# Wide matmuls over high and low x for z and three u products, state-space sums four heads at a time, scan tables two blocks at a time

## The chip, the core and the metric

The kernel runs on one core of a Trainium2 chip. The metric is the device time of one execution in microseconds. Three runs of the kernel before gave 1352.0, 1352.6 and 1353.1 us. The engines are TensorE (matmuls, in the profile PE and PEld), VectorE (DVE), ScalarE (ACT), GpSimd (POOL) and SyncE (SP, which issues most loads).

## What is computed

A decoder trunk of two layers over 256 positions of 2048 features, all in float32. Layer 0 has one input projection for two mixers, layer 1 a diagonal complex state-space mixer. Each layer ends in a residual with a layer norm. Cut to what matters here:

```
# layer 0
z, xbc, dt, q, k, v, gate = split(x @ w_in)           # z: 2048 features
xbc = silu(causal_depthwise_conv(xbc)); xs, bm, cm = split(xbc)
y   = ssd_scan(xs * dt, dt * a, bm, cm) + d_skip * xs  # 32 heads of 64 features
y_a = rms_norm(y * silu(z))
y_b = causal_attention(rotary(q), rotary(k), v) * silu(gate)   # 16 heads of 128
x   = layer_norm(alpha * x + concat(y_a, y_b) @ w_out)
# layer 1
u, gate = split(x @ w_in)                              # u: 2048 features
h_t = lam_bar * h_{t-1} + b_bar u_t                    # 128 groups of 16 channels, 64 complex states
y   = gelu(Re(C h) + d * u)
ga, gb = split(y @ w_glu)
x   = layer_norm(alpha * x + (ga * sigmoid(gb) * silu(gate)) @ w_out)
```

## The kernel before

**Products.** Nearly all the time goes into products with weights that are read once. A float32 operand is split into a high part (rounded to the matmul's replicated format, fp32r) and a low part (the rest), and a product is three matmuls: high by high, high by low and low by high. The weights come in 432 units of 512 KB (128 partitions x 1024 values: two k tiles of 512 columns). For each unit SyncE loads `raw`, ScalarE writes the high half `wh` (L230), VectorE the low half `wl` (L232). `raw`, `wh` and `wl` have four buffers each, and `split_to` is called three units ahead of the matmuls.

A "w" product (`wmm`, L297) has the weights as the stationary operand: per k tile and per 128 output features three matmuls with 256 columns, the positions, so its result is transposed (features on partitions). An "x" product (`xmm`, L276) has x stationary and 512 columns of weights moving. A product over 2048 features takes 8 units and yields 512 features, in two accumulator banks; `banks` gives two pairs in turn. B, C, xs, z, q, k, the attention gate and u are "w" products; v, the output projections, layer 1's gate and the gated unit are "x" products. The transposed x lies in two buffers, A (high) and B (low); later contents of the same kind lie in C and F.

**Other work between units.** After each unit `pump` runs jobs: `jobs` holds what the last product left to do (emptying accumulators among it), `back` holds long background work that is spread evenly over a range of units. `run` makes the instructions of a job come behind the weight splits of two units ahead on their engines. The order on each engine is at last set by a planner that simulates times when the kernel is compiled.

**State-space heads of layer 0.** `head_jobs(k)` for k = 0 to 15 treats two heads in five steps, and `skewed` runs the steps of neighbouring k staggered: `bcast` (L782: sums of log decays broadcast to all partitions by two matmuls), `decay` (ScalarE), `weigh` (VectorE), `apply` (L812, L813: the masked decay matrix times xs, full-precision float32, two heads side by side in the two 64-column halves of TensorE), `comb` (every second k: times SiLU of z). This begins in z's second product and ends in v's first.

**Tables of layer 1's scan.** `block_jobs(b)` for b = 0 to 15 makes tables from the parameters in the background of the attention and of the output projection: `bars`, `efs`, `fcs` on VectorE, `pes` (four transposes L715, eight small matmuls L719, a copy, a store to memory), `mts` on odd b (three matmuls L734).

**Layer 1.** u product 0 (`first1`) runs with the layer norm's tail. `u_store` copies a product's two banks to `ut` (ScalarE, L1104) and stores it; `u_load` brings it back in the scan's order; the scan (`enc` L1149, `rec1`, `rec2`, `dec` L1190 and L1194, `act`) runs in the background of the following products.

Of the kernel before, what the change touches and what calls it, by code (L numbers as in the profile page):

```python
# [16 lines left out]
P = 128  # L17
S = 256
# [3 lines left out]
CU = KT // UK  # L22
ALPHA = 4.0 ** 0.25
# [70 lines left out]

def _layout(inp):
# [22 lines left out]
    a["wi1"] = _chunk(f["in1_w"][0])  # L118
# [44 lines left out]
def trunk(tc, io, out):  # L163
# [8 lines left out]
    with ExitStack() as top:  # L172
# [98 lines left out]
        def xmm(ps, o, wpair, j, hk, start, stop):  # L271
            (xh, xl), k = hk
            wh, wl = wpair
            sl = slice(o * P, o * P + P)
            for i, (l, r) in enumerate(((xh, wh), (xh, wl), (xl, wh))):
                T.matmul(ps[o], l[:, k, sl], r[:, j, :], start=start and i == 0, stop=stop and i == 2)  # L276
# [3 lines left out]
        def wmm(ps, u, nu, hl, wpair, parts=WHOLE):  # L280
            pv = [p.rearrange("p (f n) -> p f n", n=S) for p in ps]
            wh, wl = wpair
            for part in parts:
                if callable(part):
                    part()
                    continue
                js, terms = part
                steps = [(j, o) for j in js for o in range(4)]
                if u == nu - 1:
                    steps = [(j, o) for o in range(4) for j in js]  # L290
                for j, o in steps:
                    first, end = u == 0 and j == 0, u == nu - 1 and j == UK - 1
                    (xh, xl), k = hl(u * UK + j)
                    sl = slice(o * P, o * P + P)
                    for i in terms:
                        l, r = ((wh, xh), (wh, xl), (wl, xh))[i]
                        T.matmul(pv[o // 2][:, o % 2, :], l[:, j, sl], r[:, k, :],  # L297
                                 start=first and i == 0 and o % 2 == 0, stop=end and i == 2 and o % 2 == 1,
                                 skip_group_check=True)

        def product(kind, hl, nu=CU, prelude=None, first=WHOLE):
# [15 lines left out]
            return ps  # L317

# [73 lines left out]
        xh = big("A", [P, KT, S], F32R)  # L392
        xl = big("B", [P, KT, S], F32R)
# [10 lines left out]
        with ExitStack() as l0:  # L404
# [35 lines left out]
            def xhl(k):  # L440
                return (xh, xl), k
# [103 lines left out]
            fmem = big("F", [P, 4096])  # L545
# [114 lines left out]
            ktp = [None]  # L660

            def block_jobs(b):
# [3 lines left out]
                def bars():  # L666
                    bc = h["bc"] = pp.tile([P, 4, 8, 16], F32, tag="bc", name=nm("bc"))
                    nc.sync.dma_start(bc.rearrange("p a g m -> p (a g m)"), io["s5bc"][b].rearrange("p a g m -> p (a g m)"))
                    bb = h["bb"] = pp.tile([P, 3, 8, 16], F32, tag="bb", name=nm("bb"))
# [10 lines left out]
                    V.tensor_scalar(bb[:, 2], bc[:, 2], nsg, None, op0=OP.mult)  # L680
# [7 lines left out]
                def efs():  # L688
                    bc, bb = h["bc"], h["bb"]
                    et = h["et"] = pp.tile([P, 8, 16, 4], F32, tag="et", name=nm("et"))  # L690
# [18 lines left out]
                def pes():  # L709
                    et, ob, bb = h["et"], h["ob"], h["bb"]  # L710
                    ev = et.rearrange("p (a i) m s -> p a (i m s)", i=2)
                    cv = bb[:, 2].rearrange("p (a i) m -> p a i m", i=2)
                    pe, pk = aux(), aux()
                    for a in range(4):
                        T.transpose(pe[:, a * P : a * P + P], ev[:, a, :], ident)  # L715
                    for a in range(4):
                        for i in range(2):
                            at = 64 * (i ^ (a % 2))
                            T.matmul(pk[at : at + 64, a * 16 : a * 16 + 16], ev[:, a, 64 * i : 64 * i + 64], cv[:, a, i, :], start=True, stop=True)  # L719
# [54 lines left out]
            def head_jobs(k):  # L774
# [40 lines left out]
                def comb():  # L815
                    if k % 2 == 1:
                        sv = sz[:, k - 1 : k + 1, :].rearrange("p f n -> p (f n)")
                        V.tensor_tensor(sv, d["y"], sv, op=OP.mult)
                        jk = c2([P, 2, S])
                        A.activation(jk.rearrange("p f n -> p (f n)"), sv, AF.Square)  # L820
                        for f in range(2):
                            G.tensor_tensor(ssq, ssq, jk[:, f, :], op=OP.add)

                return [bcast, decay, weigh, apply, comb]
# [53 lines left out]
            def attn_jobs(g, qT, kT, v, sg):  # L878
                for hp in range(2):
# [37 lines left out]
                    def pv(hp=hp, hold=hold):  # L917
# [8 lines left out]
                        if not yb:  # L926
                            yb["h"] = big("C", [P, KT, S], F32R)
                            yb["l"] = big("F", [P, KT, S], F32R)
# [32 lines left out]
            yah = big("A", [P, KT, S], F32R)  # L961
            yal = big("B", [P, KT, S], F32R)
# [11 lines left out]
            def mixhl(k):  # L974
                if k < 12:
                    return (yb["h"], yb["l"]), k
                if k < 28:
                    return (yah, yal), k - 12
                return (yb["h"], yb["l"]), k - 16

            def tailhl(k):
                return ((yb["h"], yb["l"]), k) if k < 16 else ((yah, yal), k - 16)
# [30 lines left out]
        with ExitStack() as lt:  # L1013
# [22 lines left out]
            def turned(t, f0, nf):  # L1036
                if not x1t:
                    x1t["h"] = big("C", [P, KT, S], F32R)
                    x1t["l"] = big("F", [P, KT, S], F32R)
# [42 lines left out]
            def x1hl(k):  # L1082
                return (x1t["h"], x1t["l"]), k
# [6 lines left out]
        with ExitStack() as l1:  # L1090
# [10 lines left out]
            def u_store(ps, j):  # L1101
                ut = w1("ut", [P, 4, S], 1)
# [118 lines left out]
            def y_split(j):  # L1221
                if j == 0:
                    y5["h"] = big("A", [P, KT, S], F32R)
                    y5["l"] = big("B", [P, KT, S], F32R)
# [13 lines left out]
            for j in range(8):  # L1238
                ps = product("w" if j < 4 else "x", x1hl) if j else first1
                if j < 4:  # L1240
                    jobs.append(lambda ps=ps, j=j: u_store(ps, j))
# [6 lines left out]
            def y5hl(k):  # L1248
                return (y5["h"], y5["l"]), k

            y2h = big("C", [P, KT, S], F32R)
            y2l = big("F", [P, KT, S], F32R)
# [24 lines left out]
            def y2hl(k):  # L1277
                return (y2h, y2l), k
# [7 lines left out]
        with ExitStack() as l2:  # L1286
            tp = l2.enter_context(tc.tile_pool(name="tp2", bufs=1))
            keep[0], keep[1] = tp, range(unit[0] + 2 * CU, unit[0] + 3 * CU)
            gb1 = big("A", [P, 2, D])
# [55 lines left out]
```

## Time and profile before

| | |
|---|---|
| runs before, us | 1352.0, 1352.6, 1353.1 (median 1352.6) |
| profiled execution, us | 1355.75 (span 1353.9, around it 1.85) |
| granted TensorE clock, mean | 0.996 |
| TensorE matmuls, loads of weights | 1337.0 us busy (99%), 1205.5 us (89%) |
| VectorE, ScalarE, GpSimd busy | 981.2 us (72%), 673.0 us (50%), 364.8 us (27%) |
| data moved | 283.01 MB, mean 209 GB/s |

One profiled execution is shown. Busy time of matmuls is the union of their modelled durations; since they are pipelined, the distance from one start to the next says what one costs. A group's row in the profile gives line, engine, operation, output and inputs by the program's names, shapes and count, then busy us and mean ns of one, then idle time of the engine before them and who ended it. A row of waits gives the engine and line that waited, whom it waited for, us in total, times, and the longest. In windows the five busy columns are PE, PEld, DVE, ACT, POOL, then the granted clock, the busy share of the DMA engines and GB/s.

### The profile page before, as it was taken

The numbers are of one execution on the slowest core, as the hardware profiler recorded it, in microseconds if no ns is written. First come the engines' busy times: TensorE is split into PE (matmuls) and PEld (weight loads), VectorE is DVE, ScalarE is ACT, GpSimd is POOL, SyncE is SP. The second block draws the span as 40 slices with busy tenths as digits, with TensorE's granted clock in tenths as the row PEclk, the third lists the DMA queues.
The fourth block names the chain that finished last, engine by engine and source line by source line (L and its number), as shares of the span: only waits on it lengthen the run. The fifth ranks groups of instructions, "written<-read, shape, count | busy, mean of one in ns | idle before, by whom it ended". The sixth has DMA issues, their size and how long they took to land.

```text
span 1353.9 us, 24904 instructions
## 1 busy us (share of the span) xinstructions
PE 1337.0 (99%) x9839; PEld 1205.5 (89%) x9839; DVE 981.2 (72%) x1560; ACT 673.0 (50%) x870; POOL 364.8 (27%) x648
## 2 busy tenths in 40 slices
PE   9999999999999999999999999999999999999996
PEld 8999999998998998998988888899988888888885
DVE  5767856787687879689787766748889856555556
ACT  5566567764544553554554334334444545444441
POOL 0041000122026528616798500022343100000001
PEclk9999999999999999999999999999999999999998
DMA  8655555545546756856767778497989766666762
GB/s 313 192 171 176 173 171 158 157 143 178 175 135 207 254 163 203 269 160 206 232 206 243 232 232 302 136 300 223 318 275 326 217 211 189 187 196 188 250 214 81
DMA packets 80741, 283.01 MB, mean 209 GB/s; under 512 B 9840, under 2 KB 12528, under 8 KB 80112
## 3 DMA queue, kind: packets, MB, share of 16 engines
q1 hardware_dynamic: 68112, 239.33, 56.2%
q0 software_dynamic: 7328, 30.42, 6.5%
q10 hardware_dynamic: 5184, 11.67, 2.3%
q8 instruction: 77, 1.26, 0.4%
q14 instruction: 40, 0.33, 0.1%
HBM read 260.41 MB, written 20.97 MB: 208 GB/s over the span
## 4 chain that ended last, share of the span: by engine, by line
PE 93%; DVE 4%; DMA 2%; issue 1%; ACT 0%; POOL 0%; SPq 0%; POOLq 0%; ACTq 0%; DVEq 0%
PE main L276 43%; PE main L297 42%; DVE wl L232 1%; PE aux L381 1%; PE aux L812 1%; PE aux L719 1%; PE enc L1149 1%; DMA bc<-in_s5bc 1%; PE dec L1194 1%; PE aux L924 1%; PE aux L892 1%; DMA ud<-ut 0%; PE aux L782 0%; PE dec L1190 0%; PE aux L715 0%
## 5 line engine op out<-in xcount | busy, mean ns | idle before, releaser
L232 DVE TENSOR_TENSOR wl<-raw,wh 128x1024 fp32r<-128x1024 f32 x431 | 538.4, 1251 | 323.4 <-ACT wh L230 317.4
L230 ACT ACTIVATE wh<-raw 128x1024 fp32r<-128x1024 f32 x431 | 455.8, 1059 | 580.3 <-PE main L276 269.2
L297 PE MATMUL main<-A,wh 128*128 128x256 f32 x1408 | 400.7, 285 | 1.3 <-ACT wh L230 1.1
L297 PE MATMUL main<-B,wh 128*128 128x256 f32 x1408 | 398.0, 284 | 0.0
L297 PE MATMUL main<-A,wl 128*128 128x256 f32 x1408 | 394.5, 283 | 0.0
L297 PEld LDWEIGHTS main<-A,wh 128*128 128x128 f32 x1408 | 269.7, 192 | 3.0 <-ACT wh L230 1.3
L297 PEld LDWEIGHTS main<-B,wh 128*128 128x128 f32 x1408 | 269.8, 192 | 0.4
L297 PEld LDWEIGHTS main<-A,wl 128*128 128x128 f32 x1408 | 267.8, 192 | 0.2 <-issue 0.2
L276 PE MATMUL main<-wl,A 128*128 128x512 f32 x512 | 200.5, 392 | 0.5 <-DVE wl L232 0.5
L276 PE MATMUL main<-wh,A 128*128 128x512 f32 x512 | 200.5, 392 | 0.0
L276 PE MATMUL main<-wh,B 128*128 128x512 f32 x512 | 199.9, 390 | 0.0
L276 PE MATMUL main<-wh,C 128*128 128x512 f32 x384 | 150.7, 393 | 0.0
L276 PE MATMUL main<-wh,F 128*128 128x512 f32 x384 | 149.8, 390 | 0.0
L276 PE MATMUL main<-wl,C 128*128 128x512 f32 x384 | 149.7, 390 | 0.0
L276 PEld LDWEIGHTS main<-wl,A 128*128 128x128 f32 x512 | 96.2, 188 | 21.3 <-DVE wl L232 1.8
L276 PEld LDWEIGHTS main<-wh,B 128*128 128x128 f32 x512 | 96.2, 188 | 19.9
L276 PEld LDWEIGHTS main<-wh,A 128*128 128x128 f32 x512 | 96.1, 188 | 19.8 <-issue 0.2
L653 POOL TENSOR_TENSOR c<-c 128x8 f32<-128x8 f32 (+2 forms) x192 | 106.7, 574 | 25.5 <-DMA wb<-c 18.0
L276 PEld LDWEIGHTS main<-wh,F 128*128 128x128 f32 x384 | 72.1, 188 | 15.3
L276 PEld LDWEIGHTS main<-wh,C 128*128 128x128 f32 x384 | 72.1, 188 | 15.1
L276 PEld LDWEIGHTS main<-wl,C 128*128 128x128 f32 x384 | 72.1, 188 | 14.6
L873 POOL TENSOR_TENSOR a<-a,b 64x512 f32<-64x512 f32 x16 | 28.2, 1769 | 169.1 <-DVE b L872 132.1
(279 smaller groups left out, 1651.6 us busy)
## 6 DMA issues: line engine op xcount, KB each, us to landing
raw<-in_wi SPq DMA_DIRECT2D x271, 512.0 KB, 4.0
raw<-in_wo SPq DMA_DIRECT2D x96, 512.0 KB, 4.3
raw<-in_wglu SPq DMA_DIRECT2D x64, 512.0 KB, 3.6
wt<-wb POOLq DMA_DIRECT2D x16, 896.0 KB, 6.9
wb<-ob ACTq DMA_DIRECT2D x16, 512.0 KB, 5.8
bc<-in_s5bc SPq DMA_DIRECT2D x16, 256.0 KB, 4.6
wb<-c POOLq DMA_DIRECT2D x16, 256.0 KB, 3.4
wb<-om ACTq DMA_DIRECT2D x16, 128.0 KB, 4.3
```

The lines of the kernel that those rows point to most:

```text
L230: high = A.activation(wh, raw, AF.Copy)
L232: splits[n] = (loaded[-1], high, V.tensor_tensor(wl, raw, wh.bitcast(F32), op=OP.subtract))
L276: T.matmul(ps[o], l[:, k, sl], r[:, j, :], start=start and i == 0, stop=stop and i == 2)
L297: T.matmul(pv[o // 2][:, o % 2, :], l[:, j, sl], r[:, k, :], start=first and i == 0 and o % 2 == 0, stop=end and i == 2 and o % 2 == 1, sk ...
L381: end = T.transpose(dst[:, i * P : i * P + P], s, ident)
L653: G.tensor_tensor(p[:, :, :, 0:m], cs[:, :, :, 1 : m + 1], cs[:, i, :, n : n + 1].unsqueeze(1).to_broadcast([P, 2, 4, m]), op=OP.mult)
L719: T.matmul(pk[at : at + 64, a * 16 : a * 16 + 16], ev[:, a, 64 * i : 64 * i + 64], cv[:, a, i, :], start=True, stop=True)
L812: T.matmul(yo, xs[:, 0, xc], df[:, i, 0:256], start=True, stop=False)
L873: turns.append(G.tensor_tensor(q[0:64], q[0:64], tm, op=OP.add))
L892: T.matmul(px[:, 128:384], qT[:, h, P:S], kT[:, h, :], start=True, stop=True)
L924: T.matmul(po, v[:, 0, hs], pT[:, i, 0:256], start=True, stop=False)
L1149: T.matmul(px[64 * at : 64 * at + 64, i, r * 128 + q * 64 : r * 128 + q * 64 + 64], wt[64 * i : 64 * i + 64, a * P + 64 * r : a * P + 64 * ...
```

## The change

It has four parts.

1. High and low x lie beside each other in one buffer, [128, 16, 2, 256] (`duo`): A holds what A and B held, C what C and F held. No amount of data changes.
2. z (four products) and u products 1 to 3 go through a new `product_wide`. A product is done in two halves of 256 output features. The weights of these products are stored in units of four k tiles by 256 columns, as large as before and as many. Per k tile and 128 features there are two matmuls: the high weight times 512 columns (high and low x), into both halves of a bank, and the low weight times high x, 256 columns, into the bank's second half. At the end of each half `total` copies the first half of the bank out (ScalarE) and adds the second (VectorE). z's SiLU then runs once per product, over 1024 columns; `u_store` only stores.
3. `apply` of an even k moves one step later, so that in every second step the products of four heads are issued together.
4. `pes` does nothing for even b; for odd b it does the transposes, the small matmuls, the copies and the stores of both blocks, with one accumulator and one pair of VectorE operations for the sixteen small results. `et` and the negated C table `cv` have two buffers.

```diff
+def _half(w):
+    k, n = w.shape
+    return w.reshape(k // (HK * P), HK, P, n // S, S).transpose(3, 0, 2, 1, 4).reshape(-1, P, HK * S)
...
-    cols = [xs, z]
+    cols = [_chunk(xs), _half(z)]
     for h in range(4):
-        cols += [m[:, 512 * h : 512 * h + 512] for m in (q, k, v, g)]
+        cols += [_chunk(m[:, 512 * h : 512 * h + 512]) for m in (q, k, v, g)]
     b, c = _chunk(b), _chunk(c)
     first = np.stack([b[:PAIRED], c[:PAIRED]], 1).reshape(-1, P, UK * 512)
-    a["wi0"] = np.concatenate([first, b[PAIRED:], c[PAIRED:]] + [_chunk(m) for m in cols], 0)
+    a["wi0"] = np.concatenate([first, b[PAIRED:], c[PAIRED:]] + cols, 0)
...
-    a["wi1"] = _chunk(f["in1_w"][0])
+    w = f["in1_w"][0]
+    a["wi1"] = np.concatenate([_chunk(w[:, 0:512]), _half(w[:, 512:2048]), _chunk(w[:, 2048:])], 0)
...
+        def product_wide(hl, dst, then):
+            for h in range(2):
+                ps = banks()
+                for u in range(HU):
+                    split_to(unit[0] + 3)
+                    wh, wl = (w.rearrange("p a n -> p (a n)").rearrange("p (k n) -> p k n", k=HK) for w in ready.pop(unit[0]))
+                    steps = [(j, o) for o in range(2) for j in range(HK)] if u == HU - 1 else [(j, o) for j in range(HK) for o in range(2)]
+                    for j, o in steps:
+                        first, end = u == 0 and j == 0, u == HU - 1 and j == HK - 1
+                        (xh, xl, xx), k = hl(u * HK + j)
+                        sl = slice(o * P, o * P + P)
+                        T.matmul(ps[o], wh[:, j, sl], xx[:, k, :, :].rearrange("p a n -> p (a n)"), start=first, stop=False, skip_group_check=True)
+                        T.matmul(ps[o][:, S : 2 * S], wl[:, j, sl], xh[:, k, :], start=False, stop=end, skip_group_check=True)
+                    unit[0] += 1
+                    pump(2 * HU - 1 - HU * h - u)
+
+                def total(o, ps=ps, h=h):
+                    to = dst()[:, 2 * h + o, :]
+                    A.activation(to, ps[o][:, 0:S], AF.Copy)
+                    V.tensor_tensor(to, to, ps[o][:, S : 2 * S], op=OP.add)
+
+                for o in range(2):
+                    run(lambda o=o: total(o))
+                then(h)
...
-        xh = big("A", [P, KT, S], F32R)
-        xl = big("B", [P, KT, S], F32R)
+        def duo(tag):
+            t = big(tag, [P, KT, 2, S], F32R)
+            return t[:, :, 0, :], t[:, :, 1, :], t
+
+        xh, xl, xx = duo("A")
...
+            fmem = cmem[:, 4096:8192]
...
-                    et, ob, bb = h["et"], h["ob"], h["bb"]
-                    ev = et.rearrange("p (a i) m s -> p a (i m s)", i=2)
-                    cv = bb[:, 2].rearrange("p (a i) m -> p a i m", i=2)
-                    pe, pk = aux(), aux()
-                    for a in range(4):
-                        T.transpose(pe[:, a * P : a * P + P], ev[:, a, :], ident)
-                    for a in range(4):
-                        for i in range(2):
-                            at = 64 * (i ^ (a % 2))
-                            T.matmul(pk[at : at + 64, a * 16 : a * 16 + 16], ev[:, a, 64 * i : 64 * i + 64], cv[:, a, i, :], start=True, stop=True)
-                    A.activation(ob[:, 0:512], pe, AF.Copy)
-                    if b % 2 == 0:
-                        ktp[0] = pp.tile([P, 8, 16], F32, tag="kt", name=nm("kt"))
-                    kt = ktp[0][:, 4 * (b % 2) : 4 * (b % 2) + 4, :]
-                    dc = PR("s5d")[:, 4 * b : 4 * b + 4].unsqueeze(2).to_broadcast([P, 4, 16])
-                    V.tensor_tensor(kt, C("kmask").unsqueeze(1).to_broadcast([P, 4, 16]), dc, op=OP.mult)
-                    V.tensor_tensor(kt, pk[:, 0:64].rearrange("p (a m) -> p a m", m=16), kt, op=OP.add)
-                    nc.scalar.dma_start(wb[b][:, 0:1024], ob)
+                    pair = [(b - 1, pend.pop()), (b, h)]
+                    pk = aux()
+                    kt = ktp[0] = pp.tile([P, 8, 16], F32, tag="kt", name=nm("kt"))
+                    for n, (k, d) in enumerate(pair):
+                        pe = aux()
+                        ev = d["ev"] = d["et"].rearrange("p (a i) m s -> p a (i m s)", i=2)
+                        transpose4(pe, [ev[:, a, :] for a in range(4)])
+                        A.activation(d["ob"][:, 0:512], pe, AF.Copy)
+                        nc.scalar.dma_start(wb[k][:, 0:1024], d["ob"])
+                    for n, (k, d) in enumerate(pair):
+                        cv = d["cv"].rearrange("p (a i) m -> p a i m", i=2)
+                        for a in range(4):
+                            for i in range(2):
+                                at = 64 * (i ^ (a % 2))
+                                T.matmul(pk[at : at + 64, 64 * n + a * 16 : 64 * n + a * 16 + 16], d["ev"][:, a, 64 * i : 64 * i + 64], cv[:, a, i, :], start=True, stop=True)
+                    dc = PR("s5d")[:, 4 * b - 4 : 4 * b + 4].unsqueeze(2).to_broadcast([P, 8, 16])
+                    V.tensor_tensor(kt, C("kmask").unsqueeze(1).to_broadcast([P, 8, 16]), dc, op=OP.mult)
+                    V.tensor_tensor(kt, pk[:, 0:128].rearrange("p (a m) -> p a m", m=16), kt, op=OP.add)
...
-                return [bars, efs, fcs, pes, mts] if b % 2 else [bars, efs, fcs, pes]
-
-            xs = big("C", [P, 2, D])
+                return [bars, efs, fcs, pes, mts] if b % 2 else [bars, efs, fcs, lambda: pend.append(h)]
...
-                return [bcast, decay, weigh, apply, comb]
...
+                return [bcast, decay, weigh, apply, comb] if k % 2 else [bcast, decay, weigh, lambda: None, apply]
...
-                ps = product("w", xhl)
-                for i in range(2):
-                    fs = slice(4 * j + 2 * i, 4 * j + 2 * i + 2)
-                    jobs.append(lambda ps=ps, i=i, fs=fs: A.activation(sz[:, fs, :].rearrange("p f n -> p (f n)"), ps[i], AF.Silu))
+                zs = sz[:, 4 * j : 4 * j + 4, :]
+                product_wide(xhl, lambda zs=zs: zs, lambda h, zs=zs: jobs.append(lambda: A.activation(zs, zs, AF.Silu)) if h else None)
...
+            def u_tile():
+                return w1("ut", [P, 4, S], 1)
+
+            def u_store(ut, j):
+                nc.gpsimd.dma_start(ud[j].rearrange("g a c -> (g a c)").rearrange("(f p t) -> p f t", p=P, t=S), ut)
+
+            def u_first(ps):
+                ut = u_tile()
                 for i in range(2):
                     A.activation(ut[:, 2 * i : 2 * i + 2, :].rearrange("p f n -> p (f n)"), ps[i], AF.Copy)
-                nc.gpsimd.dma_start(ud[j].rearrange("g a c -> (g a c)").rearrange("(f p t) -> p f t", p=P, t=S), ut)
+                u_store(ut, 0)
...
+                if j in range(1, 4):
+                    d = {}
+
+                    def ut(d=d):
+                        if not d:
+                            d["u"] = u_tile()
+                        return d["u"]
+
+                    product_wide(x1hl, ut, lambda h, ut=ut, j=j: jobs.append(lambda: u_store(ut(), j)) if h else None)
+                    continue
+                ps = product("x", x1hl) if j else first1
+                if j == 0:
+                    jobs.append(lambda ps=ps: u_first(ps))
```

More of the change, by code (lines that the diff above doesn't have):

```diff
@@ L22 @@
 CU = KT // UK
+HK = 4
+HU = KT // HK
 ALPHA = 4.0 ** 0.25
@@ L440, in xhl @@
             def xhl(k):
-                return (xh, xl), k
+                return (xh, xl, xx), k
             hdt = {}
@@ L815, in comb @@
                 def comb():
[L816 to L822, printed above, removed]
-                return [bcast, decay, weigh, apply, comb]
+                    sv = sz[:, k - 1 : k + 1, :].rearrange("p f n -> p (f n)")
+                    V.tensor_tensor(sv, d["y"], sv, op=OP.mult)
+                    jk = c2([P, 2, S])
+                    A.activation(jk.rearrange("p f n -> p (f n)"), sv, AF.Square)
+                    for f in range(2):
+                        G.tensor_tensor(ssq, ssq, jk[:, f, :], op=OP.add)
+                return [bcast, decay, weigh, apply, comb] if k % 2 else [bcast, decay, weigh, lambda: None, apply]
             pairy = [None]
@@ L975, in mixhl @@
                 if k < 12:
-                    return (yb["h"], yb["l"]), k
+                    return (yb["h"], yb["l"], yb["x"]), k
                 if k < 28:
-                    return (yah, yal), k - 12
-                return (yb["h"], yb["l"]), k - 16
+                    return (yah, yal, yax), k - 12
+                return (yb["h"], yb["l"], yb["x"]), k - 16
             def tailhl(k):
-                return ((yb["h"], yb["l"]), k) if k < 16 else ((yah, yal), k - 16)
+                return ((yb["h"], yb["l"], yb["x"]), k) if k < 16 else ((yah, yal, yax), k - 16)
             x1 = {}
@@ L1082, in x1hl @@
             def x1hl(k):
-                return (x1t["h"], x1t["l"]), k
+                return (x1t["h"], x1t["l"], x1t["x"]), k
             later = {1: [(1, 1)], 3: [(1, 2)], 5: [(0, 3), (1, 3)]}
@@ L1277, in y2hl @@
             def y2hl(k):
-                return (y2h, y2l), k
+                return (y2h, y2l, y2x), k
             product_pair(y5hl, finish, glu_jobs)
```

39 lines of the change are left out of this document (16 added, 23 removed).

## The prediction

> **What bounds the kernel now.** I read the page first, then who waited for whom on TensorE, then the chain of waits, and then windows and timelines of the stages that the change touches. In the page the span, the busy share of TensorE, the chain by engine, the weight split on VectorE and the two commonest matmul shapes matter:
>
> ```profile
> span 1353.9 us, 24904 instructions
> PE 1337.0 (99%) x9839; PEld 1205.5 (89%) x9839; DVE 981.2 (72%) x1560; ACT 673.0 (50%) x870; POOL 364.8 (27%) x648
> PE 93%; DVE 4%; DMA 2%; issue 1%; ACT 0%; POOL 0%; SPq 0%; POOLq 0%; ACTq 0%; DVEq 0%
> ...
> L232 DVE TENSOR_TENSOR wl<-raw,wh 128x1024 fp32r<-128x1024 f32 x431 | 538.4, 1251 | 323.4 <-ACT wh L230 317.4
> ...
> L297 PE MATMUL main<-A,wh 128*128 128x256 f32 x1408 | 400.7, 285 | 1.3 <-ACT wh L230 1.1
> ...
> L276 PE MATMUL main<-wl,A 128*128 128x512 f32 x512 | 200.5, 392 | 0.5 <-DVE wl L232 0.5
> ```
>
> The reader should see that the chain lies 93% on TensorE. Its 99% busy is by itself weak evidence, because matmuls overlap: the 285 and 392 ns are durations, not the distance between two starts. Whether it ever lacks work is told by its waits:
>
> ```profile
> PE main L297 <- DVE F L1048: 1.3, 1, 1.3
> PE enc L1149 <- DMA um<-ud: 1.3, 1, 1.3
> PE main L297 <- ACT wh L230: 1.1, 1, 1.1
> PE aux L390 <- DVE idle L385: 1.0, 1, 1.0
> PE main L276 <- DVE wl L232: 0.5, 2, 0.3
> PE main L297 <- ACT wh L222: 0.3, 1, 0.3
> ```
>
> In 1353.9 us TensorE waits 5.5 us for others. The weight halves come in time: TensorE waited twice, 0.5 us in all, for VectorE's low halves. So the time is the sum of what TensorE is given to do, and an edit is worth what it takes from that sum, as long as VectorE, ScalarE and the loads keep up. The price of a matmul I take from undisturbed stretches of the chain (start, us, what):
>
> ```profile
> 148.06 23.03 PE main L297 x192
> ...
> 810.21 48.56 PE main L276 x214
> 858.77 0.87 PE aux L381 x8
> ```
>
> A 256-column matmul takes 23.03 / 192 = 0.1199 us, a 512-column one 48.56 / 214 = 0.2269, a 128-column transpose 0.87 / 8 = 0.109. Twice the columns cost 0.107 more, so 0.1199 is 0.107 of columns and 0.013 that comes once per matmul.
>
> **Part 1, the wide products.** For z (four products) and u (products 1 to 3), each pair of a k tile and 128 output features now takes three 256-column matmuls: high weight by high x, high weight by low x, low weight by high x. After, the first two are one 512-column matmul over x's neighbouring halves. Before: 3 x 0.1199 = 0.3597. After: 0.2269 + 0.1199 = 0.3468. That saves 0.0129 us; there are 7 products x 16 k tiles x 4 feature tiles = 448 such steps, so 448 x 0.0129 = 5.8 us on the path. What is not shown in the trace is a 256-column matmul behind a 512-column one in a long run. At its least it costs its columns, 0.107, and the step saves 0.026 (11.6 us in all); if the 0.013 grew with the columns, nothing would be saved. I take 0.1199, the row of the same shape.
>
> Here the Trainium skill says something else (TensorE: Matmul & The Clock Gate, section on the back-to-back issue gap): an isolated warm matmul starts N / 2.4 ns plus 2.5 ns after the one before, which is 109 ns for 256 columns and 216 for 512. The trace disagrees, with 119.9 and 226.9 ns. By the page's fixed part this edit would save an estimated 448 x 2.5 ns = 1.1 us.
>
> Off the path each such product gains four sums (one per 128 features): a ScalarE copy of 256 columns out of the accumulator, and a VectorE add of the other 256. z also gets one SiLU over 1024 columns where two of 512 were. Loads and weight splits stay as many and as large. Rows for the sums, then the windows of z's first, second and last product, and of u products 2 and 3 (us, then busy time of each engine):
>
> ```profile
> L1261 ACT ACTIVATE gt<-main 128x256 f32<-128x256 f32 x16 | 5.1, 370 | 0.0
> L1176 DVE TENSOR_TENSOR gt<-p,p 128x256 f32<-128x256 f32 x16 | 6.6, 412 | 0.0
> L818 DVE TENSOR_TENSOR D<-aux,D 128x512 f32<-128x512 f32 x8 | 5.5, 683 | 0.0
> ...
> 153.70:177.50 23.80, 23.80 (x201) 23.80 (x201) 22.50 (x57) 12.21 (x15) 0.00 (x0) 1.00 0.58 177
> 177.50:202.10 24.60, 24.60 (x208) 24.60 (x207) 12.52 (x17) 15.66 (x23) 0.00 (x0) 1.00 0.55 167
> 228.90:256.80 27.90, 27.90 (x234) 26.16 (x233) 20.14 (x34) 20.96 (x34) 4.41 (x4) 1.00 0.51 153
> 919.70:946.60 26.90, 26.90 (x387) 26.30 (x386) 23.20 (x34) 11.11 (x12) 9.24 (x17) 1.00 0.76 234
> 946.60:972.70 26.10, 26.10 (x355) 25.70 (x354) 21.91 (x32) 10.37 (x13) 11.49 (x20) 1.00 0.89 301
> ```
>
> An add costs VectorE between 0.41 (same width, no accumulator) and 0.68 (twice the width, with one): 1.6 to 2.7 us a product. ScalarE has room in all five windows for four times 0.37. VectorE would stand at 24.1 to 25.2 of 23.0 us in z's first product, where leftover table work fills it, and at 24.8 to 25.9 of 26.1 in u's second. That is tight, but it is an average against a lead:
>
> ```profile
> DVE wl L232 <- ACT wh L230: 317.4, 239, 3.8
> ...
> ACT wh L230 <- PE main L297: 221.8, 131, 4.0
> ```
>
> VectorE's splits wait for ScalarE's high halves, and these 131 times for matmuls to give a weight buffer back. With four buffers, a split thus starts when TensorE has about three units (some 8 us) of matmuls in hand, and takes VectorE the 1.25 us of the page's L232 row. An overrun of 1 to 2 us in one product eats into that lead and returns in the next, where VectorE was busy 12.5 of 24.6 us. So I cost the sums at nothing, with that lead as their cover. Without it, every microsecond that a weight split comes later than the lead is one of TensorE.
>
> A new wait is in each sum: it is queued right behind the half's matmuls, so ScalarE and VectorE stand at it until the half ends, with the next weight split behind them. That is at most about a unit, 2.8 us, of the 8. Each half takes the other pair of accumulators, and a half lasts 4 units, 11 us, so freeing them in time asks little.
>
> **Part 2, four heads together.** The two-head products of an even step are put off by one step and join those of the odd step. Two timelines of TensorE: a step now, with the broadcast (L782) behind the heads, then a broadcast alone:
>
> ```profile
> 231.61 0.28 PE L297 MATMUL main<-A,wl 128*128 128x256 f32 x1
> 231.82 0.66 PE L812 MATMUL aux<-b,C 128*64 128x256 f32 x4
> 232.30 0.40 PE L813 MATMUL aux<-b,C 128*64 128x128 f32 x4
> 232.63 0.50 PE L782 MATMUL aux<-cumhl,sel 128*128 128x256 f32 x2
> 232.97 0.28 PE L297 MATMUL main<-A,wh 128*128 128x256 f32 x1
> ...
> 192.91 0.28 PE L297 MATMUL main<-A,wl 128*128 128x256 f32 x1
> 193.03 0.39 PE L782 MATMUL aux<-cumhl,sel 128*128 128x256 f32 x2
> 193.26 0.28 PE L297 MATMUL main<-A,wh 128*128 128x256 f32 x1
> ```
>
> The step takes 232.97 - 231.61 - 0.12 = 1.24 us from the main stream, the lone broadcast 193.26 - 192.91 - 0.12 = 0.23. What a second pair adds when full-precision matmuls follow each other without return to the main stream, attention's own products show (same widths, 256 and 128):
>
> ```profile
> 713.13 0.59 PE L924 MATMUL aux<-b,a 128*128 128x256 f32 x2
> 713.56 0.38 PE L925 MATMUL aux<-b,a 128*128 128x128 f32 x2
> 713.78 0.60 PE L924 MATMUL aux<-b,a 128*128 128x256 f32 x2
> ```
>
> The second set starts 0.65 us after the first. The kernel's two heads run side by side in two column halves, so two more heads cost 0.65. Two steps now: 2 x 1.24 = 2.48. After: 1.24 + 0.65 for four heads, 0.23 for the broadcast left alone: 2.12. It saves 0.36, eight times: 2.9 us; nothing if the heads aren't kept together. The decays of an even step are held one step longer; there are four buffers for them, and the tightest reuse waits for heads issued in the same step.
>
> **Part 3, tables in rounds of two blocks.** One block now:
>
> ```profile
> 782.64 0.39 PE L276 MATMUL main<-wh,C 128*128 128x512 f32 x1
> 782.87 0.60 PE L715 MATMUL aux<-consts,et 128*128 128x128 f32 x4
> 783.40 0.65 PE L719 MATMUL aux<-bb,et 128*64 128x16 f32 x16
> 783.97 0.50 PE L276 MATMUL main<-wl,C 128*128 128x512 f32 x1
> ```
>
> It takes 783.97 - 782.64 - 0.23 = 1.10 us. The four transposes last 0.53, of which 4 x 0.109 = 0.44 is their own, so the switch to the small matmuls costs 0.09; the way back is within the 0.57 of the small ones. Together, two blocks pay one of each. I take 0.2 us for both (0.1 to 0.3, an estimate: the way back isn't shown apart), for eight pairs 1.6 us. VectorE loses 16 small instructions. The even block's tables are stored five steps later, long before layer 1 reads them. A doubled table buffer takes a wait from VectorE that the path doesn't see.
>
> **What gives back.** The first scan step of layer 1 waits for u on its way through memory (the 1.3 us above). With u product 1 faster, TensorE comes there earlier by 13 ns for each step done since: I take 0.3 us. The layout with high and low x in one buffer moves no work.
>
> **Sum.** 5.8 + 2.9 + 1.6 - 0.3 = 10.0 us. The profiled execution took 1355.75 us, with 1353.9 of span and 1.85 around it; it would take 1345.7. The median of the three runs is 3.15 us below it at 1352.6, and the work is the same, so **1342.6 us**.
>
> **Rivals.**
> *The grouping is lost.* The order on each engine comes from a planner. If it puts main matmuls between the two pairs of heads, or between the blocks, parts 2 and 3 vanish: 5.8 - 0.3 = 5.5, 1347.1 us. Against it: in the rows above L812, L813 and L782, and L715 and L719, follow each other directly.
> *The 13 ns aren't per matmul.* If what part 1 takes out costs next to nothing, because the 13 ns go with something else than the matmul's own start, part 1 falls from 5.8 to between 0 and 1.2 and the time is 1347.3 us. Against it: one line through the two long runs of the chain gives the same 13 ns for both shapes. (The fixed part that TensorE: Matmul & The Clock Gate of the Trainium skill states lies in that span.)
> *VectorE becomes the bound (slower).* Place: ends of the wide halves in u2 and u3, and z's first. If the planner puts the sum's copy and add so early that both engines stand at them for more than the lead, TensorE stops at each of the 14 half ends. It decides from 10.0 / 14 = 0.7 us a half on; with one unit lost every other half, 7 x 2.8 = 19.6 us, 1362 us. For it: 23.20 of 26.90 us busy. Against it: the lead of three units, and only 0.5 us waited so far.
>
> **How the numbers follow.** Forecast 0.77, grouping lost 0.08, no fixed part 0.04, VectorE 0.11, of which 0.07 slower and 0.04 about even. About 0.2% (2.7 us) is what a measurement of this kernel can tell from no change. Faster: 0.77 + 0.08 + 0.04 = 0.89; same 0.04; slower 0.07. Range: at the low end a third of the extra 5.8 (11.6 - 5.8) that part 1 could bring, with tables at 0.3 a pair, 1342.6 - 1.9 - 0.8 and something for the planner's luck, 1338.5; at the high end the two rivals near 1347, with a microsecond of new waits, 1348.5.
>
> **What would show it.** The first z product to the first q product takes 103.1 us now (153.7 to 256.8); after, about 4 x 0.83 us less for the matmuls and some 2 us less for the heads. 512-column steps of 0.347 us; 9839 - 448 = 9391 matmuls; heads in eight groups of some 1.9 us, blocks in eight of some 2.0. I am wrong if TensorE's waits for VectorE or ScalarE rise by several microseconds in z or u, if a 256-column matmul behind a wide one is dearer than 0.12, or if the groups are split.

## The result and the profile after

The change gave 1346.32 us (median of 6 runs, 1344.71 to 1349.88) against 1352.66 (6 runs): a ratio of 0.9956, 95% interval 0.9943 to 0.9968. That is 6.3 us less where 10.0 were forecast, faster and inside the range. Run again beside the experiments it gave 1346.79 against 1353.24, 0.9949 (0.9937 to 0.9961), 6.5 us.

The page of the profile after, with the lines that answer to those of before, and who waited for whom on TensorE:

```profile
span 1345.0 us, 24033 instructions
PE 1328.3 (99%) x9391; PEld 1180.9 (88%) x9391; DVE 990.8 (74%) x1572; ACT 677.9 (50%) x888; POOL 369.9 (28%) x648
PE 93%; DVE 4%; DMA 1%; issue 1%; ACT 0%; SPq 0%; POOL 0%; POOLq 0%; DVEq 0%
PE main L284 43%; PE main L305 31%; PE main L338 8%; PE main L339 4%; DVE wl L240 1%; PE aux L414 1%; PE aux L851 1%; PE enc L1188 1%; PE dec L1233 1%; PE aux L763 1%; PE aux L928 1%; PE aux L960 1%; PE dec L1229 0%; PE aux L773 0%; DMA raw<-in_wi 0%
...
L338 PE MATMUL main<-A,wh 128*128 128x512 f32 x256 | 90.2, 396 | 0.8 <-DVE a L568 0.8
...
L339 PE MATMUL main<-A,wl 128*128 128x256 f32 x256 | 71.4, 280 | 0.0
...
PE main L305 <- DVE C L1081: 1.3, 1, 1.3
PE aux L773 <- DVE kt L766: 1.0, 1, 1.0
PE aux L423 <- DVE idle L418: 1.0, 1, 1.0
PE main L338 <- DVE a L568: 0.8, 1, 0.8
PE main L305 <- ACT wh L238: 0.7, 1, 0.7
PE main L284 <- DVE wl L240: 0.5, 1, 0.5
```

9391 matmuls are there as counted (256 of each new shape are z's, over A), the chain is 93% TensorE as before, and two rows of waits are new: the table matmuls L773 for VectorE's `kt`, and a wide matmul L338 for VectorE's L568, the convolution of xs. The wait of the first scan step is gone.

The two first traces differ by 8.9 us of span, more than the runs do; the execution of before took 1355.75 us, 3.1 above its median. A second trace of each kernel was taken with the experiments: spans 1350.3 before and 1344.2 after, 6.1 apart. The windows around the layer norm between the layers (columns as before, granted clock third from the end), in the trace shown in the prediction, in the first trace of the change, and in the second trace of before:

```profile
874.00:878.50 4.50, 3.93 (x20) 3.93 (x21) 3.69 (x6) 0.00 (x0) 0.17 (x1) 0.62 0.47 147
```

```profile
868.00:872.50 4.50, 3.98 (x21) 3.98 (x22) 3.64 (x6) 0.00 (x0) 0.22 (x1) 0.65 0.50 154
```

```profile
874.50:878.50 4.00, 4.00 (x36) 4.00 (x35) 3.17 (x5) 1.06 (x1) 1.06 (x3) 1.00 0.27 105
```

After the wait of the layer norm both first executions ran a stretch at half clock (0.62 and 0.65 over the windows, 0.50 from 875.2 to 878.2 us in the first of them); the second traces of both kernels did not. So this stretch is not why the first traces lie further apart. What differs is the 1.3 us wait of `enc` for `um`, which the first trace of before has alone, and the waits for weight halves (`wh` and `wl`): 1.9 us before and 1.2 after in the first traces, 1.1 and 2.1 in the second. I compare the second trace of before with the second trace of the change. Summed from each matmul's start to the next one's, in us:

| on TensorE | before | after |
|---|---|---|
| products with stationary weights | 598.4 | 437.3 + 157.4 wide = 594.7 |
| products with stationary x | 610.6 | 610.6 |
| heads and broadcasts | 20.4 | 18.1 |
| table transposes and small matmuls | 22.6 | 20.4 |
| wait of the table matmuls for `kt` | 0.25 | 1.2 |
| wait of the second half of z's first product | 0 | 0.9 |
| everything else | 85.5 | 85.8 |
| to the last matmul's start | 1337.8 | 1331.7 |

The difference is 6.1 us, near the 6.3 and 6.5 of the runs. The wait for `kt` is what the first group of table matmuls on `kt` takes, with the gap ahead of it, beyond the 0.59 us of a later group: 1.79 after, 0.84 before.

**Wide steps.** Two stretches of the second trace of the change, each over 23 steps, by the first and the last start of L338:

```profile
199.36 0.40 PE L338 MATMUL main<-A,wh 128*128 128x512 f32 x1
...
207.50 0.40 PE L338 MATMUL main<-A,wh 128*128 128x512 f32 x1
...
221.53 0.40 PE L338 MATMUL main<-A,wh 128*128 128x512 f32 x1
...
229.51 0.39 PE L338 MATMUL main<-A,wh 128*128 128x512 f32 x1
```

(207.50 - 199.36) / 23 = 0.3539 us a step, (229.51 - 221.53) / 23 = 0.3470. The second is the forecast's 0.3468, the first is not. Over all stretches only these two rhythms occur, 0.347 and 0.353 to 0.354; each stretch between two interruptions keeps one, its first steps aside.

**Heads and tables.** A step with four heads, and one round of two blocks:

```profile
213.60 0.28 PE L339 MATMUL main<-A,wl 128*128 128x256 f32 x1
213.81 0.66 PE L851 MATMUL aux<-b,C 128*64 128x256 f32 x4
214.29 0.40 PE L852 MATMUL aux<-b,C 128*64 128x128 f32 x4
214.51 0.65 PE L851 MATMUL aux<-b,C 128*64 128x256 f32 x4
214.94 0.44 PE L852 MATMUL aux<-b,C 128*64 128x128 f32 x4
...
319.86 0.66 PE L851 MATMUL aux<-b,C 128*64 128x256 f32 x4
320.35 0.39 PE L852 MATMUL aux<-b,C 128*64 128x128 f32 x4
324.11 0.66 PE L851 MATMUL aux<-b,C 128*64 128x256 f32 x4
324.59 0.39 PE L852 MATMUL aux<-b,C 128*64 128x128 f32 x4
...
419.52 0.39 PE L284 MATMUL main<-wh,A 128*128 128x512 f32 x1
419.75 1.03 PE L414 MATMUL aux<-consts,et 128*128 128x128 f32 x8
420.71 1.11 PE L763 MATMUL aux<-cv,et 128*64 128x16 f32 x32
421.75 0.50 PE L284 MATMUL main<-wh,A 128*128 128x512 f32 x1
...
427.55 0.39 PE L284 MATMUL main<-wl,A 128*128 128x512 f32 x1
428.88 0.94 PE L773 MATMUL aux<-kt,consts 128*128 128x128 f32 x6 [0.94 <-DVE kt L766]
```

The second pair of heads starts 214.51 - 213.81 = 0.70 us after the first, where 0.65 was forecast. At 320 and 324 us two pairs that belong together run apart, with main matmuls between, and so do two near 291 us. A round of two blocks takes 421.75 - 419.52 - 0.23 = 2.00 us in place of 2 x 1.10. And in that first round the next step's table matmuls, for which `kt` is not summed yet, hold TensorE: 428.88 - 427.55 is 1.33 us where a matmul's distance is 0.23, so 1.1 us, and they take 0.1 us longer themselves.

### The profile page after: what moved, and what is told of

The parts are those of the page before. It is cut to its first block, busy times and chain, and to the rows that moved or that the text cites. A ratio compares the mean times of both kernels' runs of the same rounds, so it can differ in the third digit from the quotient of the medians.

```text
span 1345.0 us, 24033 instructions
## 1 busy us (share of the span) xinstructions
PE 1328.3 (99%) x9391; PEld 1180.9 (88%) x9391; DVE 990.8 (74%) x1572; ACT 677.9 (50%) x888; POOL 369.9 (28%) x648
## 4 chain that ended last, share of the span: by engine, by line
PE 93%; DVE 4%; DMA 1%; issue 1%; ACT 0%; SPq 0%; POOL 0%; POOLq 0%; DVEq 0%
PE main L284 43%; PE main L305 31%; PE main L338 8%; PE main L339 4%; DVE wl L240 1%; PE aux L414 1%; PE aux L851 1%; PE enc L1188 1%; PE dec L1233 1%; PE aux L763 1%; PE aux L928 1%; PE aux L960 1%; PE dec L1229 0%; PE aux L773 0%; DMA raw<-in_wi 0%
## 5 line engine op out<-in xcount | busy, mean ns | idle before, releaser
L305 PE MATMUL main<-A,wh 128*128 128x256 f32 x2304 | 419.5, 285 | 0.7 <-ACT wh L238 0.7
L305 PEld LDWEIGHTS main<-A,wh 128*128 128x128 f32 x2304 | 358.9, 192 | 2.7 <-ACT wh L238 0.9
L284 PE MATMUL main<-wh,A 128*128 128x512 f32 x1024 | 321.6, 392 | 0.0
L284 PE MATMUL main<-wh,C 128*128 128x512 f32 x768 | 241.2, 392 | 0.0
L284 PEld LDWEIGHTS main<-wh,A 128*128 128x128 f32 x1024 | 191.9, 188 | 39.8 <-issue 0.3
L305 PEld LDWEIGHTS main<-A,wl 128*128 128x128 f32 x1152 | 218.9, 192 | 0.1
L284 PEld LDWEIGHTS main<-wh,C 128*128 128x128 f32 x768 | 144.1, 188 | 30.4
L338 PE MATMUL main<-A,wh 128*128 128x512 f32 x256 | 90.2, 396 | 0.8 <-DVE a L568 0.8
L338 PE MATMUL main<-C,wh 128*128 128x512 f32 x192 | 68.5, 401 | 0.0
L338 PEld LDWEIGHTS main<-A,wh 128*128 128x128 f32 x256 | 48.0, 188 | 11.8 <-ACT D L345 1.0
L339 PE MATMUL main<-C,wl 128*128 128x256 f32 x192 | 53.8, 281 | 0.0
```

Source lines behind the costliest of these rows:

```text
L305: T.matmul(pv[o // 2][:, o % 2, :], l[:, j, sl], r[:, k, :], start=first and i == 0 and o % 2 == 0, stop=end and i == 2 and o % 2 == 1, sk ...
L338: T.matmul(ps[o], wh[:, j, sl], xx[:, k, :, :].rearrange("p a n -> p (a n)"), start=first, stop=False, skip_group_check=True)
L339: T.matmul(ps[o][:, S : 2 * S], wl[:, j, sl], xh[:, k, :], start=False, stop=end, skip_group_check=True)
```

## Experiments

Each edit is shown against the change, or against the kernel before where that is said, cut to the lines that matter.

**The kernel before, unchanged.**

> The kernel before, unchanged, for a second trace of it. Theory A (its profiled execution was 3.1 us above its median through things that come and go, a stretch at half clock or the 1.3 us wait at the scan's first step, so the two traces overstate the change): this trace is shorter by 2 to 3 us, 1353 us in its own time, with one of them gone. Rival B (profiling always adds 3 us to this kernel): 1355 to 1356 us again. Time of the runs 1352.6 in both.

It took 1352.15 us in its profiled execution, 3.6 less than in the first trace, and 1353.18 in the median (ratio 0.9997, 0.9988 to 1.0006). Both the stretch at half clock and the wait at the scan's first step are gone. Theory A: the 3 us come and go.

**The wide products alone** (heads and tables as before).

```diff
-                return [bars, efs, fcs, pes, mts] if b % 2 else [bars, efs, fcs, lambda: pend.append(h)]
+                return [bars, efs, fcs, pes, mts] if b % 2 else [bars, efs, fcs, pes]
...
-                return [bcast, decay, weigh, apply, comb] if k % 2 else [bcast, decay, weigh, lambda: None, apply]
+                return [bcast, decay, weigh, apply, comb]
```

> The wide products and the shared buffer alone; heads and tables as before. Theory A (TensorE's sum decides; a wide step runs in one of two rhythms, 0.3468 or 0.3533 us, drawn anew at each restart of a stretch, mean about 0.351): 448 x (0.3597 - 0.351) = 3.9 us less, a ratio of 0.9971, and both rhythms in the trace. Rival B (the forecast's price, 0.3468 throughout): 5.8 us less, 0.9957. Rival C (the sums cost what the wide steps save): no change, 1.000, and VectorE or ScalarE named in TensorE's waits at the ends of halves.

1350.8 us against 1353.06, 0.9981 (0.9971 to 0.9991): 2.3 us less in the medians. B and C lie outside the interval, A at its edge. In the trace the products with stationary weights take 437.3 + 157.6 = 594.9 us, 3.5 less than 598.4, and 0.9 us goes back in one wait:

```profile
PE main L338 <- DVE a L568: 0.8, 1, 0.8
```

**Four heads together alone** (against the kernel before).

```diff
-                return [bcast, decay, weigh, apply, comb]
+                return [bcast, decay, weigh, apply, comb] if k % 2 else [bcast, decay, weigh, lambda: None, apply]
```

> Four heads together alone. Theory A (TensorE's sum; the planner keeps five or six of the eight groups whole): 2.3 us less by the trace of the change, a ratio of 0.9983. Rival B (the forecast's 2.9 us): 0.9979. Rival C (the longer hold of the decays makes ScalarE or VectorE late, and TensorE waits): 1.000 or above, with waits at the head products.

1350.84, 0.9981 (0.9972 to 0.999): 2.2 us less, as A and B both allow. The trace decides for A: 18.15 us in place of 20.4, with six of the eight groups whole.

**Tables in rounds of two blocks alone** (against the kernel before).

```diff
-                return [bars, efs, fcs, pes, mts] if b % 2 else [bars, efs, fcs, pes]
+                return [bars, efs, fcs, pes, mts] if b % 2 else [bars, efs, fcs, lambda: pend.append(h)]
```

> Tables in rounds of two blocks alone. Theory A: eight rounds of 2.0 us in place of sixteen of 1.1, 1.6 to 2.2 us less on TensorE, of which about 1.1 us goes into one new wait of the table matmuls L773 for VectorE's sum kt: net 0.5 to 1.1 us less, a ratio of 0.9992 to 0.9996. Rival B (no new wait; the wait belongs to the other parts of the change): 1.6 to 2.2 us less, 0.9984 to 0.9988.

1352.32, 0.9991 (0.9982 to 1.0), 0.7 us less, with an interval that reaches no change. In the trace the tables take 2.2 us less, and the wait is there with this part alone, as A has it:

```profile
PE aux L736 <- DVE kt L729: 1.4, 1, 1.4
```

The three ratios multiply to 0.9953; the whole change has 0.9956 and 0.9949. The parts add, as far as intervals of 0.001 to each side can tell.

**Wide steps in pairs.**

```diff
+                    for at in range(0, 2 * HK, 2):
+                        for low in range(2):
+                            for j, o in steps[at : at + 2]:
+                                ...  # 512-column matmuls of both steps, then the 256-column ones
```

> The change with the wide steps taken in pairs: two 512-column matmuls, then two 256-column ones. Theory A (the slow rhythm comes from a long matmul and a short one in turn): two steps take 2 x 0.3468 = 0.694 us at every place, or at most half of the stretches stay slow; TensorE has up to 448 x 0.004 = 1.8 us less than in the change, a ratio near 0.9943. Rival B (the extra 16 cycles belong to each 512-column matmul over neighbouring halves, whatever follows): two steps still take 0.707 us in most stretches, ratio 0.9956.

1345.06, 0.9941 (0.9928 to 0.9953), beside 0.9949 (0.9937 to 0.9961) for the change in the same comparison: 1.7 us apart in the medians, with overlapping intervals. The trace tells more: the wide part takes 156.2 us in place of 157.4, and two steps mostly take 0.697 us, between the two theories' 0.694 and 0.707. The pairs also changed the order of the banks: in three of four units the two steps of a pair write to different banks, in the last unit of a half to the same one. Starts from the first half of z:

```profile
161.19 0.63 PE L343 MATMUL main<-A,wh 128*128 128x512 f32 x2
...
162.58 0.63 PE L343 MATMUL main<-A,wh 128*128 128x512 f32 x2
...
165.37 0.82 PE L418 MATMUL aux<-consts,a 128*128 128x128 f32 x6
```

The last unit takes (165.37 - 162.58) / 4 = 0.697 us for two steps, the end of the unit before (162.58 - 161.19) / 2 = 0.695. So the order of lengths sets the rhythm, not the change of bank, but a part of the extra stays.

**Low weights into the other half of the bank.**

```diff
-                        T.matmul(ps[o][:, S : 2 * S], wl[:, j, sl], xh[:, k, :], start=False, stop=end, ...)
+                        T.matmul(ps[o][:, 0:S], wl[:, j, sl], xh[:, k, :], start=False, stop=end, ...)
```

> The change with the low-weight matmul added into the first half of the bank instead of the second; the sum of the two halves is the same. Theory A (the rhythm is a matter of when a stretch starts): both rhythms again, 0.347 and 0.353 us, mean 0.350 to 0.353. Rival B (the low-weight matmul waits for columns that the wide one has only just written): every step at 0.347 us, 1.8 us less than the change.

1346.33, 0.995 (0.9934 to 0.9965). Both rhythms are there again, with 157.5 us for the wide part. B falls: the columns written just before are not the cause.

**The change again.**

> The change itself, again, beside the others. Theory A: ratio 0.9956 as before, 2.5 + 2.2 + 0.7 = 5.4 to 6.3 us under the kernel before, and in its trace the two rhythms fall on other stretches than in the first trace. Rival B (the first trace's 8.9 us is the true size): 0.9934.

0.9949, as told above; A. The rhythms fell on other stretches in part: the one at 199 us was fast in the first trace and slow in the second.

**Two moves in the order of jobs.**

```diff
-                    pump(2 * HU - 1 - HU * h - u)
+                    pump(HU - 1 - u)
-                        back.extend(block_jobs(b) + [phasor_job(b)])
+                        bj = block_jobs(b)
+                        back.extend(bj[:4] + [phasor_job(b)] + bj[4:])
```

> The change with two moves in the order of jobs: what the previous product left is done within the first half of a wide product instead of over both halves, and the even matrices' step (mts) comes one job later, behind the phasors. Theory A (the new waits, 0.9 us of the first z half-turn for the convolution to leave its bank, and 1.2 us of the table matmuls for kt, are matters of job order): both are gone from the trace, 1 to 2 us less than the change, a ratio near 0.9945. Rival B (VectorE is late at both places whatever the order): the same waits or others as long, ratio 0.9956.

1343.4, 0.9925 (0.9913 to 0.9936), 3.4 us under the change. But of the two waits that theory A names only that for `kt` is gone; the wide matmul still waits 0.6 us for the convolution.

**One of the moves alone, the even matrices' step later.**

> The change with one of the two moves alone: the even matrices' step one job later, behind the phasors. Theory A (each move takes its own wait): the wait of L773 for kt, 0.9 to 1.4 us, is gone and the wait of z's second half for the convolution stays at 0.8; 1.2 to 2 us less than the change, a ratio near 0.994. Rival B (one of the moves does it all): the whole 3.4 us, 0.9925, or nothing, 0.995.

1343.64 against 1353.73, 0.9926 (0.9914 to 0.9939): this move does it all, rival B. TensorE's waits in its trace:

```profile
PE main L305 <- DVE C L1082: 1.3, 1, 1.3
PE aux L423 <- DVE idle L418: 1.0, 1, 1.0
PE main L338 <- DVE a L568: 0.8, 1, 0.8
PE main L305 <- ACT wh L230: 0.3, 1, 0.3
```

Gone are the wait for `kt` (1.2 us) and the one for a low half `wl` near 530 us (0.75 us, and 0.25 at the transposes behind it); the table part is 0.15 shorter. That is some 2.3 us. The other 0.8 that the medians suggest I can't place: the wait for the first weights at the start varies from 0.3 to 1.6 us between traces.

**VectorE's adds left out.**

```diff
                     A.activation(to, ps[o][:, 0:S], AF.Copy)
-                    V.tensor_tensor(to, to, ps[o][:, S : 2 * S], op=OP.add)
```

> The change without VectorE's 28 adds: the 256 columns of low products in each bank are left out of z and of u products 1 to 3, and ScalarE's copies alone remain. Theory A (the sums lie wholly beside TensorE's work): within 0.5 us of the change, a ratio of 0.9949 to 0.9956. Rival B (VectorE's added 11 us are partly paid on the path): 1 to 2 us less than the change, 0.994.

1345.79, 0.9943 (0.9929 to 0.9957), 0.8 us under the 0.9949 of the change. The interval holds both theories. In the trace the wide part is the same 157.4 us, and the two new waits are 0.3 us shorter each. For `kt` that proves nothing, since this wait is 0.6 us in two traces with the adds as well (pairs, other half). For the wide matmul the chain in the second trace of the change shows the add: it stands on VectorE ahead of the convolution's last operation.

```profile
165.63 0.10 DVE a L568
165.73 0.20 issue
165.93 0.42 DVE D L346
166.35 0.40 DVE a L568
166.75 0.14 issue
166.89 0.47 PE main L338
```

So the adds cost some 0.3 us at this place, and what they cost in all is not settled: the medians say 0.8 us, less than the runs can tell apart. ScalarE's copies were not taken out.

**Pairs and both moves.**

> The change with both orders: wide steps in pairs, and the two moves in the order of jobs. Theory A (they take different things from TensorE, so they add): 3.4 us and 1.2 to 1.7 us less than the change, about 1342, a ratio of 0.9915 to 0.9920 to the kernel before. Rival B (pairs gained only by another draw of the rhythms): 1343.4 as with the moves alone, 0.9925.

1342.45, 0.9917 (0.9903 to 0.993), A's size, though the interval holds B as well. The wide part takes 156.3 us and neither the wait for `kt` nor that for `wl` is there.

**The attention gate made wide as well** (on top of the pairs and both moves).

```diff
-                ps = product("w", xhl)
                 sg = a4([P, 4, S])
-                jobs.extend([lambda ps=ps, sg=sg, i=i: A.activation(sg[:, 2 * i : 2 * i + 2, :]...
+                product_wide(xhl, lambda sg=sg: sg, lambda h, sg=sg: jobs.append(lambda: A.activation(sg, sg, AF.Silu)) if h else None)
```

> The change with wide steps in pairs and the two moves in the order of jobs, and the attention gate's four products made wide as well: 256 more wide steps, four more sums to each product, where VectorE has rotary, softmax and tables to do. Theory A (TensorE's sum decides there too): 256 x (0.3597 - 0.3487) = 2.8 us less than without the gates, about 1339.7, a ratio of 0.990. Rival B (VectorE's 16 more adds and the halves' earlier need of a bank show as waits there): 1342 or more, 0.9917 or above, with TensorE's waits for VectorE or ScalarE between 330 and 670 us up by 3 us.

1341.35 against 1352.99, 0.9914 (0.99 to 0.9928); the lowest time of all, but its interval does not separate it from 0.9917. In the trace the last matmul starts 2.3 us earlier. Summed as in the table, the products take 3.0 us less, A's size, and the wait for the first weights happened to be 0.8 us shorter; the rest goes back where tables and attention break into the products. The window from 330 to 670 us, without and with the wide gates:

```profile
330.00:670.00 340.00, 340.00 (x2619) 324.27 (x2618) 274.25 (x506) 170.54 (x238) 171.83 (x323) 1.00 0.62 202
```

```profile
330.00:670.00 340.00, 339.87 (x2375) 311.86 (x2374) 280.56 (x526) 176.89 (x252) 175.69 (x323) 1.00 0.61 204
```

VectorE has 6.3 us more to do there, and TensorE is as full as before. B's waits are not there: between 330 and 670 us neither trace has a wait of TensorE that the profile lists.

## Why the prediction was right, and where its sizes were off

*What bounds the kernel.* Right: the parts went straight into the time, the tables' only just above the noise, and they add. The time lies inside the range, but 3.7 us above the point forecast, and two waits behind this were in none of its terms.

*Part 1, 5.8 us forecast.* This term was mis-sized. The wide part takes 157.4 / 448 = 0.3513 us a step, not 0.3468, because most stretches ran in the slower rhythm; it brought 3.5 to 3.7 us. The 256-column matmul takes 0.112 to 0.120 behind a wide one, no more than its row's 0.120; the wide matmul behind it takes 0.230 to 0.241 where the row of its shape has 0.227. So a part of what the step saves came back in the wide matmul. That the better rhythm has just the forecast's 0.3468 is luck: it is 0.232 and 0.115, not 0.227 and 0.120. I took a price without having seen a long run of the mixture, and the argument that one line goes through both long runs was empty, since a line goes through any two points. (By the fixed part in TensorE: Matmul & The Clock Gate of the Trainium skill, section on the back-to-back issue gap, the estimate was 1.1 us; the trace lies between that and the forecast.)

*"Each half takes the other pair of accumulators ... so freeing them in time asks little."* This failed at one place. The bank that the second half of z's first product needs still holds xs, whose convolution used to have a whole product's time, 23 us, and now has half. The convolution leaves it 0.9 us late, some 0.3 of it by the add of the first half's sum, which stands ahead of it on VectorE. Doing the convolution's jobs within the first half did not cure it; what would, was not found.

*The sums cost nothing beside the lead.* Right to about 1 us, even in the gate's products, where no new wait shows (the two experiments on sums). The lead covers the weight splits, as argued; it does not cover a bank. Of the slower rival, VectorE as the bound, came the one wait at z's first half end, 0.9 us, and nothing in u.

*Part 2, 2.9 us.* 2.3. A second pair costs 0.70 rather than 0.65, and two of the eight groups are not whole. The rival that the grouping is lost held for a quarter.

*Part 3, 1.6 us.* A whole round saves 2 x 1.10 - 2.00 = 0.2 us, as forecast, and the tables' work shrank by 2.2 in all. But in the first round the wait for `kt` grew from 0.25 to 1.2 us, which the prediction did not have: the three matmuls that use `kt` follow one step behind its sum, in order on TensorE with the main stream behind them. That was so before, too, for the odd block's half of `kt`. From the odd block's last sum of `et` to the sum of `kt` VectorE takes as long as it did (421.60 to 432.46 us before, 417.62 to 428.55 after); but TensorE comes to the three matmuls 0.8 us sooner after that sum of `et`. The forecast named who is queued behind VectorE's sums, not behind the table matmuls.

*What gives back, 0.3 us.* Not seen: the scan's wait for `um` belongs to one execution and is absent in the second trace of before as well as in both of the change.

In all 3.7 + 2.3 + 2.2 - 0.95 - 0.9 - 0.3 (the table's last line but one) = 6.1 us within rounding, where the forecast had 5.8 + 2.9 + 1.6 - 0.3.

## What to carry to other kernels

Where one engine's chain is full and hardly waits, the value of an edit is counted instruction by instruction from start-to-start distances, and separate parts add. But price a mixture of shapes by a run of that mixture if there is any, and list for each moved producer who now consumes it sooner: here two waits of about a microsecond each came from a bank wanted half a product earlier and from a sum whose readers, one step behind it, were reached sooner. Moving one job by one place in the queue gave back as much as any part of the change.

## What was not expected of the hardware

- A stream of 512- and 256-column matmuls in turn has two stable rhythms, 0.347 and 0.353 us a step, chosen anew where the stream is interrupted, and not the same in each execution. The same lengths in pairs take 0.348 on average, with single distances mostly from 0.230 to 0.236 and from 0.112 to 0.120. What picks the rhythm is open; writing to other columns did not change it.
- A stretch at half clock after the layer norm between the layers, 4.5 x (1 - 0.62) / 0.5 = 3.4 us by the window of the first trace, is there in some executions of a kernel and not in others: in the first trace of either kernel (0.62 and 0.65), not in the second (1.00).
